# A Hyena convolution as one 512-point transform over even and odd tokens, two channel chunks at once, with token tiles by parity

## Chip, cores and metric

One core of one Trainium2 chip runs the whole program as a single launch. The metric is device time in microseconds (us). The kernel before takes 1788.51 us, the median of 3 runs (1787.72 to 1789.18).

The engines are named as the profile names them: PE (TensorE) multiplies matrices from SBUF into PSUM, DVE (VectorE) and ACT (ScalarE) work element by element, POOL (GpSimd) and SP (SyncE) only issue DMA transfers here; ACT issues some too. Each engine executes its own list of instructions in order and waits at an instruction until what it needs is there.

## The reference

A bidirectional encoder block on 256 tokens of width 2048: one wide projection, a gated linear attention (GLA) branch with 4 heads, a Hyena branch of order 2, their gated sum, an output projection, and a squared-ReLU MLP, all in float32. The change is in the Hyena convolution, and in the order in which tokens lie in the tiles.

```python
def _gla_branch(...):                       # q, k, v, r by heads, decay gates la_f, la_b
    o_f = _gla_one_direction(qh, kh, vh, la_f)
    o_b = flip(_gla_one_direction(flip(qh), flip(kh), flip(vh), flip(la_b)))
    ...
def _short_conv(u, w, b):                   # 3 taps over the tokens, each channel by itself
    ...
def _hyena_branch(u, conv_w, conv_b, ...):
    uc = _short_conv(u, conv_w, conv_b).astype(f32)
    v, x1, x2 = jnp.split(uc, 3, axis=-1)
    h = _hyena_filters(L, ...)              # an MLP over 256 positions, times a decay
    filt = jnp.concatenate([h[:, :, 0], zeros, jnp.flip(h[1:, :, 1], axis=0)], axis=0)
    filt_f = jnp.fft.rfft(filt, axis=0)
    z = v
    for o, gate in enumerate((x1, x2)):
        zf = jnp.fft.rfft(z, n=2 * L, axis=1)
        zc = jnp.fft.irfft(zf * filt_f[None, :, o], n=2 * L, axis=1)[:, :L]
        z = gate * (zc + skip[o] * z)
    return z
```

## The kernel before

**Products.** Every float32 operand is split into a high part (cast on ACT, L90) and a low part (the rest, on DVE, L91), and a product is three matmuls: high x low, high x high, low x high. Weights arrive in blocks of 128x2048 (SP, L104); a block is two halves of 128x1024, each split into `whi` and `wlo`. There are three buffers of each, so ACT and DVE can run three halves ahead of PE. `next_block` takes one block for each step of a product loop.

**Order.** The loop over blocks calls `pump` after every block. `later(d, f)` puts a piece of side work on a list, to be emitted d pumps later; so side work (filters, gates, transforms) is laid between weight blocks. Within that, a scheduler sets the order on each engine at build time; marked pieces get priority or keep their place. An engine's list is then fixed.

**Stages.** In order: opening, q and k; the filter MLP and its spectra, in which the groups r, and the first of v, supply the weight work (about 100 to 265 us); GLA, beside the groups v and g1 (about 265 to 437); Hyena, beside u and go (about 437 to 890); then the gates g2, the outputs, and the MLP from about 1100 us.

**PSUM.** Two pools of four 128x512 banks: `psum_main` holds the two tiles of a token group (`v0_0`, `v0_1` and so on; group and token half), so two groups fit; `psum_side` is for side work.

**Filter stage** (`filt_time`, `filt_freq`; SBUF pool `fp`). There are 16 pairs (c, o): 8 chunks of 256 channels, 2 orders. For each, two matmul groups give `ha` and `hb`, DVE multiplies them by the decay (L433), ACT and DVE split into `hx`, and ACT copies `h0` (L441). `filt_freq` computes the spectra: `X` of even and odd positions as 128x512 products, and a third one, `X0`, from `h0` as 128x256 products (L337, L340, L341 with `eoh`, `eol`). DVE joins them into `T` (L465 to L469), which POOL stores to `Td` in DRAM (L473).

**GLA stage** (pool `gp`, opened when `fp` is closed, and placed in its memory). For each head a group `v` of four blocks; its two PSUM tiles are split at once, with priority, into `yg`, a tile of the base pool. `gla_gates` loads `wr` (ACT's queue, L542), splits it into `ws` (L544, L545) and multiplies `z` (L556); ACT and DVE make the gates.

**Hyena stage** (pool `hp`). For each s of 4 (512 channels) the groups `uv`, `ux1`, `ux2` give v, x1 and x2; `short_conv` multiplies PSUM by the taps (six 512-wide products, L734), adds the bias (L736) and shifts tokens by accumulating DMAs on POOL (L743). Then, for each of the two chunks c of s and each order o: `hy_load` (POOL loads T as `Tl`), `hy_fwd` (transform on PE to `Zp`, ACT copies to `Z`), `hy_mul` (DVE: L785 to L791, then a split), and `hy_inv` (inverse transform to `yp`, gate on DVE, L806, then a split, or the transposes `yT` at the last order).

Of the kernel before, what the change touches and what calls it, by code (L numbers as in the profile page):

```python
# [47 lines left out]
def block_kernel(  # L48
# [301 lines left out]
    def filt_consts():  # L350
        raw = fp.tile([P, 4, P], F32, tag="w4", bufs=2, name="dftraw")
# [22 lines left out]
    def filt_layer(l):  # L374
        def run():
            mw, mc, g = fst["mw"], fst["mc"], fst["g"]
            with tc.high_priority():
# [15 lines left out]
                g2 = fp.tile([P, L], F32, tag="dec", bufs=2, name=f"mlpg{l}")  # L393
# [16 lines left out]
    def filt_time(c, o):  # L410
        def run():
            l1, l2 = fst["l"]
            if o == 0:
                dec = fp.tile([P, NT, CW], F32, tag="dec", bufs=2, name=f"dec{c}")
                nc.scalar.dma_start(dec, decay_in[:, c * CW:(c + 1) * CW].rearrange("(a p) d -> p a d", p=P))
                fst["dec"] = dec
# [6 lines left out]
            nc.scalar.activation(wb, w4[:, 1, :], AF.Copy, scale=sgn_sb[:, 1:2])  # L423
# [13 lines left out]
            hx = fp.tile([P, 2, 2, 2, CW], F32R, tag="hx", bufs=2, name=f"hx{c}{o}")  # L437
            split_hi_lo(hx[:, 0], hx[:, 1], h)
            h0 = fp.tile([P, 2, 2, CW], F32R, tag="h0", bufs=1, name=f"h0_{c}{o}")
            for d in range(2):  # L440
                nc.scalar.copy(h0[d * 64:d * 64 + 64], hx[0:64, :, :, d].bitcast(F32))  # L441
            fst[("h", c, o)] = (hx, h0)
        return run

    def filt_freq(c, o):
        def run():
            hx, h0 = fst.pop(("h", c, o))
            eoh, eol = fst["eo"]
            par_ps = []
            for par in range(2):  # L450
                pt = psum_side(f"X{c}{o}{par}")
                mm3(pt, eoh[:, par], eol[:, par], hx[:, 0, par], hx[:, 1, par], True, True)
                par_ps.append(pt.rearrange("p (a b) -> p a b", a=2))
            xe, xo = par_ps
            t = fp.tile([P, 2, 3, CW], F32, tag="T", bufs=2, name=f"T{c}{o}")
            e, e0 = t[:, 0, 2:0:-1], t[:, 0, 0]
            nc.scalar.copy(e, xe)
# [4 lines left out]
            nc.scalar.copy(e0, p0[:, 0:CW])
            TT = nc.vector.tensor_tensor
            for sg, op in ((1, ALU.subtract), (0, ALU.add)):
                TT(t[:, sg, 2:0:-1], e, xo, op=op)  # L465
            for sg, op in ((1, ALU.subtract), (0, ALU.add)):
                TT(t[:, sg, 0], e0, p0[:, CW:], op=op)
            TT(t[:, :, 2], t[:, :, 2], t[:, :, 0], op=ALU.subtract)
            nc.vector.scalar_tensor_tensor(t[:, :, 1], t[:, :, 1], sgn_sb[:, 0:1], t[:, :, 0],  # L469
                                           op0=ALU.mult, op1=ALU.subtract)  # L470
            td = drp.tile([P, 2, 3, CW], F32, tag=f"T{c}{o}", name=f"Td{c}{o}")
            for ri in range(2):
                nc.gpsimd.dma_start(td.rearrange("(s p) r k c -> r p s (k c)", s=2)[ri],  # L473
                                    t[ri * 64:ri * 64 + 64].rearrange("p s k c -> p s (k c)"))
            T_dram[(c, o)] = td
        return run
# [14 lines left out]
    nc.vector.tensor_tensor(a_sum[:, 0], pa[:, 0], a_low, op=ALU.add)  # L491
# [134 lines left out]
    def gla_scores(h):  # L626
        def run():
# [21 lines left out]
            split_hi_lo(sth, stl, st)  # L649
# [79 lines left out]
    def short_conv(pss, i, tag, name):  # L729
        y = hp.tile([P, NT, 512], F32, tag=tag, bufs=2 if tag == "x2" else 1, name=name)  # L730
# [28 lines left out]
    def hy_load(c, o):
        def run():  # L760
            t = hp.tile([P, 2, 3, CW], F32, tag="Tl", name=f"Tl{c}{o}")
            nc.gpsimd.dma_start(t, T_dram[(c, o)])
            cst[("T", c, o)] = t
        return run

    def hy_fwd(c, o):
        def run():
            t = cst.pop(("T", c, o))
            zh, zl = cst.pop(("z", c, o))
            z = hp.tile([P, 3, 2, CW], F32, tag="Z", name=f"Z{c}{o}")  # L770
            for ri in range(2):
                pz = psum_side(f"Zp{c}{o}{ri}")
                mm3(pz.rearrange("p (a b) -> p a b", a=2), dfth[:, ri], dftl[:, ri], zh, zl, True, True, hold=True)
                nc.scalar.copy(z[:, 2:0:-1, ri, :], pz.rearrange("p (a b) -> p a b", a=2))
            cst[("Z", c, o)] = (t, z)
        return run

    def hy_mul(c, o):
        def run():
            t, z = cst.pop(("Z", c, o))  # L780
            a = hp.tile([P, 3, 2, CW], F32, tag="pa", name=f"pa{c}{o}")
            b = hp.tile([P, 3, 2, CW], F32, tag="pb", name=f"pb{c}{o}")
            TT = nc.vector.tensor_tensor
            full = [P, 3, 2, CW]
            TT(z[:, 0], z[:, 1], z[:, 2], op=ALU.add)  # L785
            TT(a, z, t[:, 0, :, None, :].broadcast_to(full), op=ALU.mult)
            TT(b, z[:, :, ::-1, :], t[:, 1, :, None, :].broadcast_to(full), op=ALU.mult)
            TT(a[:, :, 0], a[:, :, 0], b[:, :, 0], op=ALU.subtract)
            TT(a[:, :, 1], a[:, :, 1], b[:, :, 1], op=ALU.add)
            y = a[:, 1:3]  # L790
            TT(y, y, a[:, 0:1].broadcast_to([P, 2, 2, CW]), op=ALU.add)  # L791
            yh = hp.tile([P, 2, 2, CW], F32R, tag="pb", name=f"Yh{c}{o}")
            yl = hp.tile([P, 2, 2, CW], F32R, tag="Yl", name=f"Yl{c}{o}")
            split_hi_lo(yh, yl, y)
            cst[("Y", c, o)] = (yh, yl)
        return run

    def hy_inv(c, o):
        def run():
            yh, yl = cst.pop(("Y", c, o))  # L800
            py = psum_side(f"yp{c}{o}")
            py3 = py.rearrange("p (a b) -> p a b", a=2)
            mm3(py3, dfth[:, 2], dftl[:, 2], yh[:, :, 0], yl[:, :, 0], True, False)
            mm3(py3, dfth[:, 3], dftl[:, 3], yh[:, :, 1], yl[:, :, 1], False, True)
            zf = hp.tile([P, NT, CW], F32, tag="zf", name=f"zf{c}{o}")
            nc.vector.tensor_tensor(zf, py3, gate_part(("x1", "x2")[o], c), op=ALU.mult)  # L806
            if o == 0:
                z = tuple(hp.tile([P, NT, CW], F32R, tag=t, name=f"{t}{c}") for t in ("zh", "zl"))
                split_hi_lo(z[0], z[1], zf)
                cst[("z", c, 1)] = z  # L810
            else:
                pt = psum_side(f"yT{c}")
                for cc in range(2):
# [821 lines left out]
```

## Time and profile before

| what | us |
|---|---|
| median of the runs | 1788.51 |
| span of the profiled execution | 1785.8 |
| PE busy | 1778.0 |
| DVE busy | 1482.7 |
| ACT busy | 1052.2 |
| POOL busy | 180.0 |

The median lies 2.7 us above the span; the difference is what lies around the profiled program. A row of the groups reads: line, engine, operation, output and inputs by name (partitions by elements, type), count, then the busy time, the mean time of one in ns, and the idle time of the engine just before it with what ended it. A row of the timeline begins with start and duration in us; `x2` joins two instructions, and an idle time stands in brackets. A row of the windows gives the stretch, its length, the busy time of PE, weight loads, DVE, ACT and POOL with the instructions in brackets, PE's granted clock, the share of DMA time and GB/s. Busy times of neighbouring instructions overlap on PE and DVE, so the pace, from start to start, is shorter than the duration.

### The profile page before, as it was taken

Reading aid. Unit: us, or ns where it says so; the run is one execution under the profiler, and the core shown is the slowest. Engines: PE = TensorE matmul, PEld = TensorE weight load, DVE = VectorE, ACT = ScalarE, POOL = GpSimd, SP = SyncE. Lnnn points to the kernel's source line nnn. Section 1 sums busy time; section 2 is a strip of 40 time slices with the busy share of each in tenths; the row PEclk is TensorE's granted clock in tenths of the full one; section 3 lists DMA queues with packets and bytes.
Section 4 is the critical chain, followed back from the end, with each engine's and each line's share of the span. In section 5 each row is a group of like instructions: output and inputs, shape, how many; then the busy total and the mean of one; then the engine's idle time right before and its main releaser. Section 6 shows DMA issues by size and latency. Waiting matters only on the chain.

```text
span 1785.8 us, 23513 instructions
## 1 busy us (share of the span) xinstructions
PE 1778.0 (100%) x8739; PEld 1500.6 (84%) x8739; DVE 1482.7 (83%) x1919; ACT 1052.2 (59%) x1418; POOL 180.0 (10%) x234
## 2 busy tenths in 40 slices
PE   9999999999999999999999999999999999999998
PEld 7888888888888888888888889888888888888887
DVE  6789886885679998898755558889999999999998
ACT  6578767875344444444544445676666666666663
POOL 1011110000011201011000000011111111111110
PEclk9999999999999999999999999999999999999999
DMA  8668776445797979798555664687888787888864
GB/s 325 236 241 292 262 233 202 148 165 206 230 288 254 290 232 292 262 289 253 215 184 186 245 263 163 224 247 242 276 248 252 246 264 241 278 240 249 262 217 167
DMA packets 81586, 428.95 MB, mean 240 GB/s; under 512 B 10072, under 2 KB 12648, under 8 KB 40768
## 3 DMA queue, kind: packets, MB, share of 16 engines
q1 hardware_dynamic: 47664, 336.35, 50.5%
q0 software_dynamic: 26608, 71.18, 19.6%
q10 hardware_dynamic: 7200, 19.93, 3.1%
q8 instruction: 68, 1.11, 0.3%
q14 instruction: 46, 0.38, 0.1%
HBM read 383.96 MB, written 16.25 MB: 224 GB/s over the span
## 4 chain that ended last, share of the span: by engine, by line
PE 96%; DVE 3%; DMA 0%; issue 0%; ACT 0%; SPq 0%; DVEq 0%
PE f L151 12%; PE f L155 6%; PE w L1266 5%; PE w L1265 5%; PE w L1264 5%; PE g L202 3%; PE g L201 3%; PE g L203 3%; PE ux L203 3%; PE ux L202 3%; PE ux L201 3%; PE r L201 2%; PE r L203 2%; PE r L202 2%; PE k L151 2%; PE v L202 2%
## 5 line engine op out<-in xcount | busy, mean ns | idle before, releaser
L90 ACT CAST whi<-raw 128x1024 fp32r<-128x1024 f32 x360 | 379.1, 1054 | 382.6 <-PE ux L203 89.3
L91 DVE TENSOR_TENSOR wlo<-raw,whi 128x1024 fp32r<-128x1024 f32 x360 | 438.0, 1220 | 186.5 <-ACT whi L90 183.4
L151 PE MATMUL f<-hT,whi 128*128 128x512 f32 x984 | 243.9, 391 | 0.0
L151 PEld LDWEIGHTS f<-hT,whi 128*128 128x128 f32 x984 | 180.8, 188 | 35.0
L1122 DVE TENSOR_TENSOR wlo<-fraw,whi 128x1024 fp32r<-128x1024 f32 x112 | 136.7, 1221 | 14.3 <-ACT whi L1125 11.0
L155 PEld LDWEIGHTS f<-hT,wlo 128*128 128x128 f32 x984 | 126.2, 191 | 4.8
L155 PE MATMUL f<-hT,wlo 128*128 128x256 f32 x984 | 127.7, 283 | 0.0
L1125 ACT CAST whi<-ring 128x1024 fp32r<-128x1024 f32 x56 | 59.1, 1055 | 113.1 <-DVE ring L1122 113.1
L1185 POOL DMA_DIRECT2D ring<-wblk x56 | 48.6, 868 | 722.6 <-DVE ring L1122 722.6
L1125 ACT CAST whi<-fraw 128x1024 fp32r<-128x1024 f32 x112 | 117.7, 1051 | 0.0
L1125 ACT CAST b_h<-ring 128x1024 fp32r<-128x1024 f32 x112 | 87.9, 834 | 24.0 <-PE w L1266 21.9
L202 PE MATMUL g<-wlo,xT 128*128 128x512 f32 x256 | 100.1, 391 | 0.0
L203 PE MATMUL ux<-whi,xT 128*128 128x512 f32 x256 | 99.9, 390 | 0.0
L203 PE MATMUL g<-whi,xT 128*128 128x512 f32 x256 | 99.9, 390 | 0.0
L202 PE MATMUL ux<-wlo,xT 128*128 128x512 f32 x256 | 99.6, 389 | 0.0
L201 PE MATMUL g<-whi,xT 128*128 128x512 f32 x256 | 93.8, 392 | 0.0
L201 PE MATMUL ux<-whi,xT 128*128 128x512 f32 x256 | 89.7, 389 | 0.0
L1122 DVE TENSOR_TENSOR ring<-ring 128x512 f32<-128x512 f32 x112 | 77.0, 687 | 1.9
L1122 DVE TENSOR_TENSOR b_l<-ring,b_h 128x1024 fp32r<-128x1024 f32 x56 | 68.3, 1219 | 9.1 <-ACT b_h L1125 9.0
L1122 DVE TENSOR_TENSOR wlo<-ring,whi 128x1024 fp32r<-128x1024 f32 x56 | 68.6, 1224 | 2.6 <-ACT whi L1125 0.6
L1122 DVE TENSOR_TENSOR fa<-ring,fa 128x1024 fp32r<-128x1024 f32 x56 | 68.2, 1217 | 0.0
L1186 POOL DMA_DIRECT2D ring<-ring x56 | 67.6, 1207 | 0.0
(515 smaller groups left out, 4299.5 us busy)
## 6 DMA issues: line engine op xcount, KB each, us to landing
raw<-wblk SPq DMA_DIRECT2D x188, 1024.0 KB, 5.3
fraw<-wblk SPq DMA_DIRECT2D x56, 1024.0 KB, 4.8
ring<-wblk SPq DMA_DIRECT2D x56, 1024.0 KB, 6.7
ring<-wblk POOLq DMA_DIRECT2D x56, 256.0 KB, 4.4
ring<-ring POOLq DMA_DIRECT2D x56, 256.0 KB, 5.0
Td<-T POOLq DMA_DIRECT2D x32, 384.0 KB, 5.4
conv_sb<-conv_rows SPq DMA_DIRECT2D x12, 1024.0 KB, 11.5
Tl<-Td POOLq DMA_DIRECT2D x16, 768.0 KB, 9.2
```

Of the source, the lines that this page charges most:

```text
L90: return (nc.scalar.copy(hi, src), nc.vector.tensor_tensor(lo, src, hi.bitcast(F32), op=ALU.subtract))
L91: nc.vector.tensor_tensor(lo, src, hi.bitcast(F32), op=ALU.subtract))
L151: MM(ps[:, :, ts], hi[:, js], act[:, kt, :, ts], start=(kt == 0 and opens), stop=(kt == KT - 1))
L155: MM(ps[:, 0, ts], lo[:, js], act[:, kt, 0, ts], start=False, stop=False)
L201: order(MM(pss[tb], sh, wh, start=(kt == ends[0]), stop=False))
L202: order(MM(pss[tb], sh, wl, start=False, stop=False))
L203: order(MM(pss[tb], sl, wh, start=False, stop=(kt == ends[1])))
L1122: return pin(nc.vector.tensor_tensor(dst, a, b, op=op))
L1125: return pin(nc.scalar.copy(hi, src))
L1264: pin(MM(ps, sh, wh, start=(p == begin), stop=False))
L1265: MM(ps, sh, wl, start=False, stop=False)
L1266: pin(MM(ps, sl, wh, start=False, stop=(p == end - 1)))
```

## The change

The 512-point transform of a sequence of 256 tokens is now taken as one transform over even tokens and one over odd tokens (`Ze`, `Zo`), whose sum and difference are the two halves of the spectrum. The filter's spectrum is built from taps modulo 4: four products of 128x256 for each pair, in place of two of 128x512 and two of 128x256 (each of three matmuls). One T holds each spectrum for both halves of the frequencies, for two chunks, as one tile of 1 MB, so 8 loads of 1 MB take the place of 16 of 768 KB. The Hyena steps work on 512 channels at once: each is called 8 times, for (s, o), and was called 16 times, for (c, o).

For this, the token tiles lie by parity: tile 0 holds even tokens, tile 1 odd ones, from the input on. GLA needs tokens in order, so the sums of q, k and a are written in order by a stride, and each head's v takes a new way: ACT copies PSUM to `vm`, POOL's queue moves it by four transfers to `vr` in order, and the split into `yg` follows two pumps later. The scores are turned to parity order in their split. x2 and the decay have one buffer where there were two; the filter's multiplication by the decay is one product of 1024; the products with T are 2048 wide.

```diff
@@ filt_time
-            h = fp.tile([P, 2, 2, CW], F32, tag="h", bufs=1, name=f"h{c}{o}")
-            for par, pp in ((0, pa), (1, pb)):
-                nc.vector.tensor_tensor(
-                    h[:, par], pp.rearrange("p (a b) -> p a b", a=2),
-                    dec[:, par, None, :].broadcast_to([P, 2, CW]), op=ALU.mult,
-                )
...
+            nc.scalar.copy(h[top, 1:4:2], pa[top])
+            nc.scalar.copy(h[end, 1:4:2], pa[end, ::-1])
+            for r, src in ((0, top), (2, end)):
+                for d, dst in enumerate((top, end)):
+                    nc.scalar.copy(h[dst, r], pb[src, d])
+            nc.vector.tensor_tensor(h, h, dec, op=ALU.mult)
...
@@ filt_freq
+            near, far = (psum_side(f"X{c}{o}{i}").rearrange("p (a c) -> p a c", a=2) for i in range(2))
+            for ps, r0 in ((near, 0), (far, 2)):
+                for i in range(2):
+                    mm3(ps[:, i], eoh[:, r0 + i], eol[:, r0 + i], hx[:, 0, r0 + i], hx[:, 1, r0 + i], True, True)
+            f = fp.tile([P, 2, CW], F32, tag="F", name=f"F{c}{o}")
+            nc.scalar.copy(f, near)
+            TT = nc.vector.tensor_tensor
+            u = fp.tile([P, 4, CW], F32, tag="U", name=f"U{c}{o}")
+            TT(u[:, 0:4:2], f, far, op=ALU.add)
+            TT(u[:, 1], f[:, 0], far[:, 0], op=ALU.subtract)
+            TT(u[top, 3], f[end, 1], far[end, 1], op=ALU.subtract)
+            TT(u[end, 3], far[top, 1], f[top, 1], op=ALU.subtract)
+            t = fp.tile([P, 2, 2, CW], F32, tag="T", bufs=2, name=f"T{c}{o}")
+            TT(t[:, :, 0], u[:, 0:2], u[:, 2:4], op=ALU.add)
+            TT(t[:, :, 1], u[:, 0:2], u[:, 2:4], op=ALU.subtract)
...
@@ the heads' v
+        mixed = gp.tile([P, NT, 512], F32, tag="vm", name=f"vm{h}")
         with tc.high_priority():
             for tb in range(NT):
-                split_hi_lo(vh[:, tb], vl[:, tb], pss[tb])
-        v_sb[h] = (vh, vl)
+                nc.scalar.copy(mixed[:, tb], pss[tb])
+        rows = gp.tile([P, NT, 512], F32, tag="vr", name=f"vr{h}")
+        for b in range(NT):
+            for tb in range(NT):
+                nc.gpsimd.dma_start(rows[tb:P:2, b], mixed[b * 64:(b + 1) * 64, tb])
+
+        def split(h=h, vh=vh, vl=vl, rows=rows):
+            split_hi_lo(vh, vl, rows)
+            v_sb[h] = (vh, vl)
+        later(2, split)
@@ short_conv
-        y = hp.tile([P, NT, 512], F32, tag=tag, bufs=2 if tag == "x2" else 1, name=name)
+        y = hp.tile([P, NT, 512], F32, tag=tag, name=name)
...
-            (y[1:P], past[0:P - 1]),
-            (y[0:1, 1], past[P - 1:P, 0]),
-            (y[0:P - 1], ahead[1:P]),
-            (y[P - 1:P, 0], ahead[0:1, 1]),
+            (y[:, 1], past[:, 0]),
+            (y[1:P, 0], past[0:P - 1, 1]),
+            (y[:, 0], ahead[:, 1]),
+            (y[0:P - 1, 1], ahead[1:P, 0]),
...
@@ hy_fwd, hy_mul, hy_join, hy_split, hy_inv
+            for ri in range(2):
+                even, odd = psum_side(f"Ze{s}{o}{ri}"), psum_side(f"Zo{s}{o}{ri}")
+                for ps, i in ((even, 0), (odd, 1)):
+                    mm3(ps, dfth[:, 2 * i + ri], dftl[:, 2 * i + ri], zh[:, i], zl[:, i], True, True, hold=True)
+                e = b[:, ri, 0:512]
+                nc.scalar.copy(e, even)
+                for k, op in enumerate((ALU.add, ALU.subtract)):
+                    nc.vector.tensor_tensor(x[:, ri, :, k], halves_of(e), halves_of(odd), op=op)
...
+            for dst, src, ri in ((a, x, 0), (b, x[:, ::-1], 1)):
+                nc.vector.tensor_tensor(dst, src, t[:, ri:ri + 1].broadcast_to([P, 2, 1024]), op=ALU.mult)
...
+            TT(a[:, 0], a[:, 0], b[:, 0], op=ALU.subtract)
+            TT(a[:, 1], a[:, 1], b[:, 1], op=ALU.add)
+            y = a.rearrange("p r (h k c) -> p (r h) k c", h=2, k=2)
+            w = hp.tile([P, 2, 4, CW], F32, tag="X", name=f"W{s}{o}")
+            for i, op in enumerate((ALU.add, ALU.subtract)):
+                TT(w[:, i], y[:, :, 0], y[:, :, 1], op=op)
...
@@ the Hyena loop
-                steps = [(2 * s + j % 2, j // 2, 4 * j) for j in range(4)]
-                for c, o, d in steps:
-                    later(7 + d, hy_load(c, o))
-                    later(9 + d, hy_fwd(c, o))
-                for c, o, d in steps:
-                    later(13 + d, hy_inv(c, o))
-                for c, o, d in steps:
-                    later(9 + d, hy_mul(c, o))
+                for o in range(2):
+                    for d, step in ((5, hy_load), (8, hy_fwd), (9, hy_mul), (10, hy_join), (12, hy_split), (14, hy_inv)):
+                        later(d + 8 * o, step(s, o))
```

Three places show how the lists of the engines move.

PE where the filter stage ends. Before, the last spectrum's products (`X710`, `X711`, their third part `X071`) stand inside block 37, in the second group of v:

```order
L201 MATMUL v1_1_2678<-whi37_1_2582,xT_82 128x512
L337 MATMUL X710_2155<-hx71_2071,eoh_351 128x512
L340 MATMUL X710_2155<-hx71_2071,eoh_351 128x512
L341 MATMUL X710_2155<-hx71_2071,eol_352 128x512
L337 MATMUL X711_2159<-hx71_2071,eoh_351 128x512
...
L203 MATMUL v1_1_2678<-whi37_1_2582,xT_82 128x512
L337 MATMUL X071_2165<-h0_71_2074,eoh_351 128x256
L340 MATMUL X071_2165<-h0_71_2074,eoh_351 128x256
...
L201 MATMUL v1_0_2677<-whi37_1_2582,xT_82 128x512
```

After, the spectrum of that pair stands behind the whole second group of v, directly ahead of the third group, `v2`:

```order
L208 MATMUL v1_1_2706<-whi40_1_2747,xT_82 128x512
L209 MATMUL v1_1_2706<-wlo40_1_2748,xT_82 128x512
L210 MATMUL v1_1_2706<-whi40_1_2747,xT_82 128x512
L344 MATMUL X710_2180<-hx71_2099,eoh_351 128x256
L347 MATMUL X710_2180<-hx71_2099,eoh_351 128x256
L348 MATMUL X710_2180<-hx71_2099,eol_352 128x256
...
L344 MATMUL X711_2181<-hx71_2099,eoh_351 128x256
...
L348 MATMUL X711_2181<-hx71_2099,eol_352 128x256
L208 MATMUL v2_0_3001<-whi41_0_2872,xT_82 128x512
```

The last spectrum moved down by about three and a half weight blocks, from inside group v1 to its end.

ACT at the same place. Before, the casts that free the PSUM tiles of v0 (`yg` from `v0_0` and `v0_1`) stand ahead of the copies of the last T; the casts for v1 come after the scan and gate loads (`scan_sb`, `wr`) and several halves of weights:

```order
L90 CAST yg_2406<-v0_0_2413 128x512
L90 CAST yg_2406<-v0_1_2414 128x512
L90 CAST whi38_0_2612<-raw38_2610 128x1024
L90 CAST whi38_1_2616<-raw38_2610 128x1024
L457 COPY T71_2163<-X710_2155 128x2x256
L462 COPY T71_2163<-X071_2165 128x256
...
L531 DMA scan_sb_2409<-scan_in 128x260
L542 DMA wr0_2449<-wa2 128x512
...
L544 CAST ws0_2451<-wr0_2449 128x512
...
L90 CAST yg_2406<-v1_0_2677 128x512
L90 CAST yg_2406<-v1_1_2678 128x512
```

After, the spectrum's copy `F71` is followed by the copies of group v0 out of PSUM, then the scan and gate loads, then the copies of group v1:

```order
L90 CAST whi42_0_2961<-raw42_2959 128x1024
L462 COPY F71_2194<-X710_2180 128x512
L695 COPY vm0_2697<-v0_0_2437 128x512
L695 COPY vm0_2697<-v0_1_2438 128x512
L533 DMA scan_sb_2433<-scan_in 128x260
L544 DMA wr0_2473<-wa2 128x512
L546 CAST ws0_2475<-wr0_2473 128x512
L544 DMA wr1_2775<-wa2 128x512
L695 COPY vm1_2993<-v1_0_2705 128x512
L695 COPY vm1_2993<-v1_1_2706 128x512
L90 CAST yg_2430<-vr0_2700 128x1024
L90 CAST whi42_1_2965<-raw42_2959 128x1024
```

The rows that free the PSUM tiles of v0 moved from before the last spectrum to behind it, and the gate loads and the next half of weights behind them.

DVE in the Hyena stage, between two halves of weights (`wlo`). Before, around the second chunk's products of order 1 (`pa11`, `pb11`) and the convolution of x2:

```order
L786 TENSOR_TENSOR pa11_5324<-Z11_5297,Tl11_5212 128x1536
L787 TENSOR_TENSOR pb11_5325<-Z11_5297,Tl11_5212 128x1536
L91 TENSOR_TENSOR wlo91_1_5270<-raw91_5263,whi91_1_5269 128x1024
L788 TENSOR_TENSOR pa11_5324<-pa11_5324,pb11_5325 128x3x256
L789 TENSOR_TENSOR pa11_5324<-pa11_5324,pb11_5325 128x3x256
L91 TENSOR_TENSOR wlo92_0_5339<-raw92_5336,whi92_0_5338 128x1024
L791 TENSOR_TENSOR pa11_5324<-pa11_5324 128x1024
L91 TENSOR_TENSOR wlo92_1_5343<-raw92_5336,whi92_1_5342 128x1024
...
L734 TENSOR_TENSOR cx21_5447<-ux21_0_5261,conv_sb_4257 128x512
L734 TENSOR_TENSOR shift_4258<-ux21_0_5261,conv_sb_4257 128x512 x2
...
L91 TENSOR_TENSOR wlo94_0_5416<-raw94_5413,whi94_0_5415 128x1024
...
L736 TENSOR_TENSOR cx21_5447<-cx21_5447,conv_sb_4257 128x1024
```

After, around the products of (1, 0) and the convolution of x2:

```order
L91 TENSOR_TENSOR wlo94_0_5439<-raw94_5436,whi94_0_5438 128x1024
L790 TENSOR_TENSOR X10_5470<-pb10_5471,Zo100_5473 128x2x256 x2
...
L801 TENSOR_TENSOR pa10_5544<-X10_5470,Tl10_5338 128x2048
L801 TENSOR_TENSOR pb10_5471<-X10_5470,Tl10_5338 128x2048
L91 TENSOR_TENSOR wlo94_1_5443<-raw94_5436,whi94_1_5442 128x1024
L746 TENSOR_TENSOR cx21_5496<-ux21_0_5302,conv_sb_4305 128x512
...
L746 TENSOR_TENSOR shift_4306<-ux21_0_5302,conv_sb_4305 128x512
...
L91 TENSOR_TENSOR wlo95_0_5513<-raw95_5510,whi95_0_5512 128x1024
L809 TENSOR_TENSOR pa10_5544<-pa10_5544,pb10_5471 128x1024
L810 TENSOR_TENSOR pa10_5544<-pa10_5544,pb10_5471 128x1024
L748 TENSOR_TENSOR cx21_5496<-cx21_5496,conv_sb_4305 128x1024
L91 TENSOR_TENSOR wlo95_1_5517<-raw95_5510,whi95_1_5516 128x1024
```

The products are 2048 wide instead of 1536 and stand with four adds ahead of them; between `wlo94_0` and `wlo95_1` stand the adds, the products, the six products of the convolution, two joins and the bias add.

More of the change, by code (lines that the diff above doesn't have):

```diff
@@ L446, in run @@
         def run():
-            hx, h0 = fst.pop(("h", c, o))
+            hx = fst.pop(("h", c, o))
             eoh, eol = fst["eo"]
[L449 to L455, printed above, removed]
@@ L466, in run @@
[L466 to L471, printed above, removed]
+            top, end = slice(0, 64), slice(64, P)
+            near, far = (psum_side(f"X{c}{o}{i}").rearrange("p (a c) -> p a c", a=2) for i in range(2))
@@ L752, in run, with halves_of @@
-            for i in range(2):
-                cst[("z", 2 * s + i, 0)] = tuple(t[:, :, i * CW:(i + 1) * CW] for t in z)
-        return run
-    def gate_part(n, c):
-        return cst[(n, c // 2)][:, :, c % 2 * CW:(c % 2 + 1) * CW]
-    def hy_load(c, o):
+            t = hp.tile([P, 2, 1024], F32, tag="Tl", name=f"Tl{s}{o}")
+            nc.gpsimd.dma_start(t, T_dram[(s, o)].rearrange("p r h s c -> p r (h s c)"))
+            cst[("T", s, o)] = t
+        return run
+    def halves_of(ap):
+        return ap.rearrange("p (h c) -> p h c", h=2)
@@ new lines, in hy_fwd, with run @@
+    def hy_fwd(s, o):
+        def run():
+            zh, zl = cst.pop(("z", s, o))
+            x = hp.tile([P, 2, 2, 2, CW], F32, tag="X", name=f"X{s}{o}")
+            b = hp.tile([P, 2, 1024], F32, tag="pb", name=f"pb{s}{o}")
+            for ri in range(2):
[6 more added lines that the diff above has]
+                    nc.vector.tensor_tensor(x[:, ri, :, k], halves_of(e), halves_of(odd), op=op)
+            cst[("X", s, o)] = (x, b)
+        return run
@@ new lines, in hy_split, with run, hy_inv @@
+    def hy_split(s, o):
+        def run():
+            w = cst.pop(("W", s, o)).rearrange("p i (r h) c -> p (i r) (h c)", r=2)
+            yh, yl = (hp.tile([P, 4, 512], F32R, tag=t, name=f"{n}{s}{o}") for t, n in (("pb", "Yh"), ("pa", "Yl")))
+            split_hi_lo(yh, yl, w)
+            cst[("Y", s, o)] = (yh, yl)
+        return run
+    def hy_inv(s, o):
+        def run():
+            yh, yl = cst.pop(("Y", s, o))
+            g = cst.pop((("x1", "x2")[o], s))
+            for i in range(2):
+                py = psum_side(f"yp{s}{o}{i}")
+                for ri in range(2):
+                    k = 2 * i + ri
+                    mm3(py, dfth[:, 4 + k], dftl[:, 4 + k], yh[:, k], yl[:, k], ri == 0, ri == 1)
+                nc.vector.tensor_tensor(g[:, i], py, g[:, i], op=ALU.mult)
+            if o == 0:
+                split_input(s, 1, g)
+            else:
+                for i in range(2):
+                    later(1 + 2 * i, hy_turn(2 * s + i, g[:, :, i * CW:(i + 1) * CW]))
+        return run
@@ L760, in run, with hy_turn @@
+    def hy_turn(c, zf):
         def run():
[L761 to L813, printed above, removed]
-                    for tb in range(NT):
-                        nc.tensor.transpose(pt[:, cc * L + tb * P:cc * L + (tb + 1) * P], zf[:, tb, cc * P:(cc + 1) * P], ident)
-                pt = pt.rearrange("p (a b) -> p a b", a=2)
-                if c >= NCH - 2:
-                    split_hi_lo(yhT[:, 2 * c:2 * c + 2, 0], yhT[:, 2 * c:2 * c + 2, 1], pt)
-                    return
-                yo = base.tile([P, 2, L], F32, tag="sum", name=f"yo{c}")
-                nc.scalar.copy(yo, pt)
-                def keep():
-                    yd = drp.tile([P, 2, L], F32, tag=f"yd{c}", name=f"yd{c}")
-                    nc.gpsimd.dma_start(yd, yo)
-                    yh_dram[c] = yd
-                later(1, keep)
@@ new lines, in run @@
+            pt = psum_side(f"yT{c}")
+            for cc in range(2):
+                for tb in range(NT):
+                    nc.tensor.transpose(pt[:, cc * L + tb * P:cc * L + (tb + 1) * P], zf[:, tb, cc * P:(cc + 1) * P], ident)
+            pt = pt.rearrange("p (a b) -> p a b", a=2)
+            if c >= NCH - 2:
+                split_hi_lo(yhT[:, 2 * c:2 * c + 2, 0], yhT[:, 2 * c:2 * c + 2, 1], pt)
+                return
+            yo = base.tile([P, 2, L], F32, tag="sum", name=f"yo{c}")
@@ L828, in hy_inv, with keep @@
+            nc.scalar.copy(yo, pt)
+            def keep():
+                yd = drp.tile([P, 2, L], F32, tag=f"yd{c}", name=f"yd{c}")
+                nc.gpsimd.dma_start(yd, yo)
+                yh_dram[c] = yd
+            later(1, keep)
         return run
@@ L1603, in _layout @@
     emb = np.zeros((P, L), f)
-    by_parity = np.concatenate([np.arange(0, L, 2), np.arange(1, L, 2)])
-    emb[:33] = emb[64:97] = e.T[:, by_parity]
+    emb[:33] = emb[64:97] = e.T[:, times]
     dl = np.abs(np.linspace(math.log(1e-2) / 1.5, math.log(1e-2) / 0.3, D, dtype=f))
-    decay = np.exp(-t * dl[None, :]).astype(f)[by_parity]
+    decay = np.exp(-t * dl[None, :]).astype(f)
+    decay = np.stack([decay[abs(np.concatenate(rows[r]))] for r in range(4)], axis=1)
     up = np.triu(np.ones((64, 64), np.int32))
```

125 lines of the change are left out of this document (70 added, 55 removed).

## The prediction

> **What bounds the kernel now.** I read the page's first and fourth parts, then the view of waits for TensorE, then the table of windows by stage.
>
> ```profile
> span 1785.8 us, 23513 instructions
> PE 1778.0 (100%) x8739; PEld 1500.6 (84%) x8739; DVE 1482.7 (83%) x1919; ACT 1052.2 (59%) x1418; POOL 180.0 (10%) x234
> PE 96%; DVE 3%; DMA 0%; issue 0%; ACT 0%; SPq 0%; DVEq 0%
> ...
> PE warm L272 <- DVE ones_sb L334: 1.5, 1, 1.5
> PE open L296 <- ACT whi-1_2_133 L308: 0.9, 1, 0.9
> ...
> 437.00:880.00 443.00, 443.00 (x1967) 366.72 (x1966) 374.91 (x374) 201.41 (x220) 54.74 (x74) 1.00 0.83 263
> 265.00:437.00 172.00, 172.00 (x851) 143.26 (x850) 124.94 (x241) 125.92 (x258) 1.77 (x3) 1.00 0.51 179
> 100.00:265.00 165.00, 165.00 (x771) 137.09 (x770) 147.33 (x200) 121.72 (x155) 18.03 (x30) 1.00 0.77 262
> ```
>
> TensorE (PE) is busy for the whole span and the chain runs through it for 96%. The two waits listed are all that it has, 2.4 us in the opening. In the filter stage (100 to 265 us), the GLA stage (265 to 437) and the Hyena stage (437 to 880; these three hold the change) it is busy in every microsecond at a granted clock of 1.00. So the time is TensorE's work, and the rule for the sum is simple: a matmul removed is worth its pace; anything removed from DVE, ACT or the DMA queues is worth nothing; and anything that makes TensorE wait costs all of that wait. DVE at 374.91 of 443 us is 85% of the Hyena stage, so bursts matter there, not averages. The profiled span is 1785.8 us and the median of the runs 1788.5, so 2.7 us lie around the span; the sum is made on the span and these are added.
>
> **TensorE's own work.** The paces come from the chain, where rows stand start to start, and the counts from the groups by form.
>
> ```profile
> 63.31 1.91 PE k L155 x16
> 65.22 3.65 PE k L151 x16
> ...
> L337 PE MATMUL X<-hx,eoh 128*128 128x512 f32 x32 | 12.7, 397 | 0.0
> L337 PE MATMUL X<-h,eoh 128*128 128x256 f32 x32 | 9.0, 280 | 0.0
> ```
>
> Sixteen 256-column matmuls take 1.91 us (0.1195 each), sixteen of 512 take 3.65 (0.228; 0.2265 between undisturbed starts). The spectrum of a filter pair was 6 matmuls of each size (three lines, 32 of each in all); it becomes 12 of 256. That is 6 x 16 x (0.2265 - 0.1195) = **10.3 us less**. Everything else on TensorE keeps its columns: the transform was two 512-wide products over two chunks and is now two over even and odd tokens at twice the width half as often. 1785.8 - 10.3 = 1775.5 is the floor.
>
> **Filter stage, DVE.**
>
> ```profile
> L465 DVE TENSOR_TENSOR T<-T,X 128x512 f32<-128x512 f32 x32 | 21.8, 681 | 1.7 <-ACT T L457 1.4
> L91 DVE TENSOR_TENSOR hx<-h,hx 128x1024 fp32r<-128x1024 f32 x16 | 19.5, 1219 | 0.5 <-ACT hx L90 0.5
> L467 DVE TENSOR_TENSOR T<-T,X 128x256 f32<-128x256 f32 x32 | 13.3, 415 | 4.7 <-ACT T L462 4.4
> L469 DVE SCALAR_TENSOR_TENSOR T<-T,sgn_sb 128x512 f32<-128x512 f32 x16 | 11.9, 745 | 0.0
> L468 DVE TENSOR_TENSOR T<-T 128x512 f32<-128x512 f32 x16 | 11.0, 687 | 0.2
> ```
>
> By those sizes a pair loses two 512 products (1.36) for one of 1024 (1.22), and 2 x 0.681 + 2 x 0.415 + 0.687 + 0.745 = 3.62 becomes three of 512 and three of 256 elements, 3.29. DVE gets 0.5 us a pair lighter while TensorE gets 0.64 lighter: its load stays near 147.33 of 165 us, and I expect no wait from it. ACT's small copies replace two 1.05 us casts; its cover is 121.72 of 165. Cost taken: 0.
>
> **The joint between filter and GLA stage.** Here the change's new copy is decisive. The value tiles were split straight from PSUM into a base tile; now they are first copied into vm, a tile of the GLA pool, which takes memory of the filter pool. That copy must wait until the last spectrum T has been stored by DMA. Before, only an unimportant DVE instruction waited for this:
>
> ```profile
> 265.51 0.74 DVE L469 SCALAR_TENSOR_TENSOR T<-T,sgn_sb 128x512 f32<-128x512 f32 x1
> ...
> 266.55 1.20 POOL L473 DMA_DIRECT2D Td<-T  x2 [12.67 <-DVE T L469]
> ...
> 272.24 0.17 DVE L534 TENSOR_SCALAR nba_sb<-ba_sb 128x16 f32<-128x16 f32 x1 [2.22 <-DMA Td<-T]
> ...
> 272.66 0.46 ACTq L542 DMA_DIRECT2D wr<-wa  x1
> ...
> 277.92 0.62 ACT L544 CAST ws<-wr 128x512 fp32r<-128x512 f32 x1 [3.66 <-DMA wr<-wa]
> ...
> DMA to landing us min/median/max: 3.6/5.4/8.7
> ```
>
> From the end of T (266.25) to the first instruction that the landing lets through (272.24) are 6.0 us, 0.3 of them to the issue; the last row, of the Td stores, gives 3.6 to 8.7 for the landing. In the new order the copies of v0 out of PSUM stand on ACT behind F71 and that wait; TensorE's next tile v2_0 needs v0's PSUM buffer (four buffers: v0, v1). The last spectrum's matmuls stand directly ahead of v2_0, after all of v1: there is nothing left to run under the wait.
>
> With t = 0 at the start of X710: twelve matmuls, TensorE free at 1.43. F71 is copied by 1.8; DVE does wlo42_0 until 2.5, then U71 (0.6 + 3 x 0.335) until 4.1 and T71 (2 x 0.6) until 5.3. (0.6 and 0.335 are 681 and 415 ns less the 80 ns by which neighbours overlap.) The landing comes 5.9 later, at 11.2, the copy (580 ns for 512 elements, as L457 takes below) ends at 11.8, and v2_0 starts at 11.9.
>
> ```profile
> L457 ACT COPY T<-X 128x512 f32<-128x512 f32 x16 | 9.3, 580 | 6.0 <-DMA Td<-T 5.2 <-PE X L341 0.7
> ```
>
> **Wait: 11.9 - 1.43, about 10.4 us**; bounds 9.0 to 14.1 by landings of 3.6 and 8.7 against the 5.0 of this one (its second store was issued at 267.15). What is late next stands behind the same copies on ACT: scan, wr0, ws0, wr1, vm1, yg, whi42_1. wr0 is issued at 12.7 and lands 5.2 later (272.66 to 277.92), ws0 is ready at 19.3, and z00, which TensorE reaches after 26 products at 17.8, waits 1.6. vm1, yg and whi42_1 follow until 22.5, wlo42_1 until 24.0 against 22.35 wanted: 1.7. ws1 waits for wr1, so wlo43_0 comes at 28.1 against 26.7: 1.4. These **follow-ups are 4.7 us**, bounds 0 (a fast landing of wr0 and ACT catching up) to 6.
>
> The clock: in the tail of this run, where TensorE's last matmul ends at about 1780.5, the records show the clock falling.
>
> ```profile
> 1782.00:1786.00 4.00, 0.00 (x0) 0.00 (x0) 0.00 (x0) 0.00 (x0) 0.00 (x0) 0.67 0.42 130
> ```
>
> A mean of 0.67, if it fell to one half, means a fall near 1783.3, some 3 us into idleness (an estimate from this row). So the 10.4 us wait should end at a lower clock. I add nothing for it: v2_0 and its neighbours run slower, but they only run up to z00, which has 1.6 us to wait anyway. The Trainium skill ("TensorE: Matmul & The Clock Gate", in "Part 1: The HAM clock gate", "What's actually happening") puts the fall at an idle window of about 3.4 us and the return to full rate after about 3.4 us of busy time; by it the first 3.4 us at half rate would cost an estimated 1.7 us, hence at most 0.1 us more than that wait hides.
>
> The sixteen vr copies go through POOL's queue at about 0.6 us each; 1.77 of 172 us of POOL and half of the DMA time are used in the GLA stage, and their split comes two weight blocks (10.9 us) later, against 2.4 us of issues and 5.4 of landing. Cost taken: 0, bound 2.
>
> **Hyena stage.** DVE must deliver a half weight block (wlo) every 2.72 us (12 x 0.2265), and TensorE has three halves in buffers. What decides is how much other work stands between two deliveries. Rows of the stage before:
>
> ```profile
> 540.83 1.75 DVE L786 TENSOR_TENSOR pa<-Z,Tl 128x1536 f32<-128x1536 f32 x1
> 542.49 1.75 DVE L787 TENSOR_TENSOR pb<-Z,Tl 128x1536 f32<-128x1536 f32 x1
> 544.16 0.68 DVE L91 TENSOR_TENSOR zl<-zf,zh 128x512 fp32r<-128x512 f32 x1
> 544.76 1.22 DVE L91 TENSOR_TENSOR wlo<-raw,whi 128x1024 fp32r<-128x1024 f32 x1
> 545.90 0.95 DVE L788 TENSOR_TENSOR pa<-pa,pb 128x768 f32<-128x768 f32 x1
> ...
> 549.91 1.22 DVE L91 TENSOR_TENSOR wlo<-raw,whi 128x1024 fp32r<-128x1024 f32 x1
> ...
> 552.57 0.39 PE L202 MATMUL uv<-wlo,xT 128*128 128x512 f32 x1
> ```
>
> Paces are 1.66 (1536), 1.14 (1024) and 0.60 (512). The half that ends at 551.13 is first used at 552.57: 1.44 us to spare, near the least of the stage, after a burst of 512 + 512 + 2 x 1536 + 512. The change has less DVE work in sum (13312 elements of transform work for each s instead of 15360) but twice as much at a time: four adds, two products of 2048, four joins of 1024. A 2048-wide product appears in no row; between 1.66 (1536) and 2.27 (two of 1024) I take 2.20, on the line through 1024 and 1536.
>
> For s = 1, 2, 3 with o = 0 the order puts adds and products, then six convolution products, then two joins and the bias add between neighbouring halves. t = 0 at the first Ze product: TensorE needs 2.72 for Ze and Zo, 5.43 for block 93, 0.44 for the transposes yT1, 5.44 for block 94, and wants wlo95_0 at 14.26. DVE: wlo94_0 until 2.45, adds (4 x 0.6) 4.85, products (4.4) 9.25, wlo94_1 10.4, convolution (6 x 0.6) 14.0, wlo95_0 15.1, with the semaphore 15.3: **1.0 late**. Joins and bias (3 x 1.14) and wlo95_1 until 19.8 against 18.0: **1.8 late**. With 0.3 for rounding at the two hand-overs, 3.1 us three times, 9.3. At (0,0) and at o = 1 of s = 0, 1, 2 the same sum with convolution, adds and products gives a half at about 15.2 against 14.3, 0.85 us four times, 3.4. At (3,1) no convolution stands near: 0. **Hyena sum 12.7 us**; with products at 1.66 each burst is 1.1 lighter (6.0 left at the three places, none at the four), with 2.27 about 1 us more in all.
>
> **Sum.** 1785.8 - 10.3 + 10.4 + 4.7 + 12.7 = 1803.3 us of span, plus 2.7: **1806 us**. Its own bounds: low terms 9.0 + 0 + 6.0 give 1793.2, high ones 14.1 + 6 + 2 + 13.7 give 1814.0.
>
> **Rivals.**
> 1. *The bursts are covered.* The three buffered halves swallow them: DVE runs ahead further than my sum lets it. For it: 1.44 us to spare is the worst row shown of before; against it: before's largest excess of DVE over TensorE across three halves is 3.5 us by my paces, the new one 8.9, and the buffers give about 5.9. Time 1806 - 12.7 = 1793.
> 2. *Not slower: the joint does not hold TensorE.* One mechanism: if the last Td store lands before v0's copy is due, ACT frees the PSUM buffer at once and the queue behind it is on time. Price 10.4 + 4.7, time 1791, within 0.2%. It decides if the landing comes within about 1.4 us of X711, that is before DVE could even have finished T71 at 5.3; the row of 3.6 us at best speaks against it.
> 3. *Only the removed matmuls count.* Rivals 1 and 2 together: 1778. TensorE's order and the idle shares of DVE (15%) and ACT (over 40%) speak for it, the two walks against it.
> 4. *More waits than I see*: the filter's pairs are stretched over four more weight blocks with one buffer for decay and h, so an ACT or DVE wait could reach TensorE in the filter stage too, or the clock stays low through the three follow-ups: 10 us more, 1816 and above.
>
> **How the numbers follow.** Forecast 0.60, of which all is slower; rival 1 0.12 (0.05 of it inside the band, the rest slower), rival 2 0.09 (0.07 inside), rival 3 0.11 (faster), rival 4 0.08. A difference of 0.2% is about what a measurement of this kernel can tell from none, so the band is 1784.9 to 1792.1. Faster 0.11, same 0.12, slower 0.77. The range leaves out rival 3 and the far part of rival 4: 1788 to 1817.
>
> **What would show it.** Right: the view of waits lists TensorE on v2_0 waiting for ACT's vm copy, once, about 10 us, the clock below 1.00 behind it; small waits on z00, whi42_1 and wlo43_0; and in 437 to 890 us some ten waits of 0.5 to 2 us for wlo. X groups show 192 matmuls of 256 columns. Wrong: TensorE still at 100% busy in the Hyena windows (rival 1), no wait at v2_0 (rival 2), or waits in 100 to 265 us (rival 4).

## The result, and the profile after

The changed kernel takes 1802.06 us, the median of 4 runs (1801.57 to 1802.23), against 1788.12 us for the kernel before on the same chip. The ratio is 1.0076, with a 95% interval of 1.0062 to 1.0091: **slower by 13.9 us**. The forecast was 1806 us, within 1788 to 1817.

The page of the changed kernel:

```profile
span 1800.2 us, 23526 instructions
PE 1774.5 (99%) x8739; PEld 1495.6 (83%) x8739; DVE 1460.3 (81%) x1871; ACT 1051.7 (58%) x1442; POOL 185.2 (10%) x242
```

The view of waits of its TensorE (PE); the columns are engine and line, what it waited for, us in total, times, the longest:

```profile
PE v L208 <- ACT vm L695: 9.6, 1, 9.6
PE go L209 <- DVE wlo L91: 7.0, 7, 1.5
PE ux L209 <- DVE wlo L91: 1.7, 3, 0.6
...
PE g L209 <- DVE wlo L91: 0.4, 1, 0.4
...
PE v L209 <- DVE wlo L91: 0.4, 1, 0.4
```

PE is no longer busy throughout. DVE's busy time fell from 1482.7 to 1460.3 us, which bought nothing. PE's own went from 1778.0 to 1774.5 only, although the spectra became 11 us cheaper. The windows show where PE idles, and a part of why its busy time fell so little:

```profile
264.00:270.00 6.00, 5.74 (x32) 4.80 (x30) 3.02 (x4) 2.65 (x3) 0.00 (x0) 1.00 0.73 217
...
272.00:274.00 2.00, 0.00 (x0) 0.00 (x0) 1.76 (x4) 0.00 (x0) 0.00 (x0) 0.96 0.10 41
274.00:276.00 2.00, 0.00 (x0) 0.00 (x0) 0.00 (x0) 0.00 (x0) 1.20 (x2) 0.50 0.41 88
...
280.00:282.00 2.00, 2.00 (x6) 1.55 (x5) 0.00 (x0) 0.02 (x1) 1.61 (x4) 0.50 0.96 287
282.00:284.00 2.00, 2.00 (x6) 1.58 (x5) 0.68 (x1) 0.60 (x1) 0.00 (x0) 0.50 0.44 154
284.00:286.00 2.00, 2.00 (x10) 1.59 (x10) 0.00 (x0) 1.71 (x3) 0.00 (x0) 0.98 0.42 131
```

PE idles from 269.75 to 279.31. The granted clock is at 0.50 from just before 274, and still for 4.8 us after PE has resumed: from 280 to 284 PE counts as fully busy but the row counts 6 matmuls in each 2 us, and 10 in the 2 us behind them. A busy share doesn't show such a loss; the clock beside it does. PE's timeline over the same stretch:

```profile
279.31 0.79 PE L208 MATMUL v<-whi,xT 128*128 128x512 f32 x1 [9.56 <-ACT vm L695]
...
280.32 0.63 PE L210 MATMUL v<-whi,xT 128*128 128x512 f32 x1
280.75 0.63 PE L208 MATMUL v<-whi,xT 128*128 128x512 f32 x1
...
284.14 0.39 PE L210 MATMUL v<-whi,xT 128*128 128x512 f32 x1
284.37 0.39 PE L208 MATMUL v<-whi,xT 128*128 128x512 f32 x1
```

Eleven matmuls start in the 4.83 us up to 284.14, 0.43 apart, then 0.23 apart; at full pace they take 2.49, so 2.3 us are lost. (By the means of 0.96 and 0.98 the clock fell 4.1 us into the idle time and rose 4.8 us after its end, estimates from these rows. The Trainium skill, in "TensorE: Matmul & The Clock Gate", "What's actually happening", asks for at least one idle window of about 3.4 us before the fall and at least one busy window of that length before the rise, and says that the windows run freely; 4.1 and 4.8 us agree with that.)

The timeline of the joint, a start and a duration first in each row, an idle time in brackets:

```profile
273.12 0.68 DVE L471 TENSOR_TENSOR T<-U 128x512 f32<-128x512 f32 x1
274.10 1.20 POOL L477 DMA_DIRECT2D Td<-T  x2 [12.02 <-DVE T L471]
278.53 0.17 DVE L536 TENSOR_SCALAR nba_sb<-ba_sb 128x16 f32<-128x16 f32 x1 [4.72 <-DMA Td<-T]
278.67 0.59 ACT L695 COPY vm<-v 128x512 f32<-128x512 f32 x1 [8.63 <-issue]
...
279.07 0.46 ACTq L544 DMA_DIRECT2D wr<-wa  x1
...
281.98 0.62 ACT L546 CAST ws<-wr 128x512 fp32r<-128x512 f32 x1 [2.24 <-DMA wr<-wa]
```

This is the forecast chain: T ends at 273.80, its store lands at 278.53, the copy of v0 starts at 278.67, and v2_0 at 279.31. In this timeline ACT's wait is marked "issue"; DVE's nba_sb, let through at the same moment, names the landing, and so does the view of the tile Td, where the copy stands among those that waited for the store:

```profile
  ACT vm L695: 8.6, 1
```

That the copy waits because vm lies in memory of the closed filter pool is read from the code: vm and T have nothing else to do with each other. No run put vm elsewhere. wr0 then came in 2.9 us, where it had taken 5.2 before.

DVE in one of the three bursts of the Hyena stage (s = 1, o = 0), and the two late halves behind it (a late half is a half weight block whose wlo is not ready when PE wants it):

```profile
615.04 2.29 DVE L801 TENSOR_TENSOR pa<-X,Tl 128x2048 f32<-128x2048 f32 x1
617.25 2.28 DVE L801 TENSOR_TENSOR pb<-X,Tl 128x2048 f32<-128x2048 f32 x1
619.45 1.22 DVE L91 TENSOR_TENSOR wlo<-raw,whi 128x1024 fp32r<-128x1024 f32 x1
620.58 1.28 DVE L746 TENSOR_TENSOR cx<-ux,conv_sb 128x512 f32<-128x512 f32 x2
621.78 2.47 DVE L746 TENSOR_TENSOR shift<-ux,conv_sb 128x512 f32<-128x512 f32 x4
624.17 1.22 DVE L91 TENSOR_TENSOR wlo<-raw,whi 128x1024 fp32r<-128x1024 f32 x1
...
625.44 0.50 PE L209 MATMUL go<-wlo,yg 128*128 128x512 f32 x1 [0.64 <-DVE wlo L91]
...
629.99 0.50 PE L209 MATMUL go<-wlo,yg 128*128 128x512 f32 x1 [1.51 <-DVE wlo L91]
```

DVE works without a gap through all its rows here and delivers the half at 625.39; PE takes it at 625.44, after 0.64 us of idle time, and the next half after 1.51.

Each wait costs PE more than its idle time, since the start before it and the one behind it are stretched too. So the balance is made from start to start: the time from each matmul's start to the next one's, added up over the 8739 matmuls of both traces by the name of the output. The groups that differ by more than 0.4 us:

```
                     before    after   difference (us)
X                     33.66    32.19      -1.47   (of the after, 9.72 is the wait behind the last X)
v                     87.43    90.52      +3.08
g1, g2               175.67   176.79      +1.11
go                    87.12    96.59      +9.47
ux                   174.51   177.19      +2.68
s (128x64)             6.93     7.45      +0.53
w                    304.71   305.33      +0.62
r                     87.97    87.55      -0.41
```

So X itself saves 33.66 - 22.47 = 11.2 us; the wait at v2_0 costs 9.7, what follows it 3.1 (v) + 0.5 (s, the scores) and about 1 in g1, and the Hyena stage 12.15 (go and ux).

### The profile page after: what moved, and what is told of

Its sections match the earlier page's. It is cut to its first block, busy times and chain, and to the rows that moved or that the text cites. A ratio compares the mean times of both kernels' runs of the same rounds, so it can differ in the third digit from the quotient of the medians.

```text
span 1800.2 us, 23526 instructions
## 1 busy us (share of the span) xinstructions
PE 1774.5 (99%) x8739; PEld 1495.6 (83%) x8739; DVE 1460.3 (81%) x1871; ACT 1051.7 (58%) x1442; POOL 185.2 (10%) x242
## 4 chain that ended last, share of the span: by engine, by line
PE 88%; DVE 9%; issue 2%; ACT 1%; DMA 0%; DVEq 0%; ACTq 0%
PE f L151 12%; PE f L155 6%; PE w L1295 5%; PE w L1294 5%; PE w L1293 5%; PE g L209 3%; PE g L210 3%; PE g L208 3%; PE ux L209 3%; PE ux L210 3%; PE ux L208 2%; DVE wlo L91 2%; PE k L151 2%; PE r L210 2%; PE r L209 2%
```

## The experiments

The kernel before took 1788.12 us beside the changed kernel, 1788.30 beside the runs with 20/15, 19/15, a product left out and the finer steps, and 1788.67 beside the others. So a difference to the changed kernel's 1802.06 us holds to about half a microsecond.

**The joint: the filter pairs laid closer.** Two kernels, with

```diff
-        n = 4 + (i * 21) // 15
+        n = 4 + (i * 20) // 15
```

and with 19 in place of 20. The last spectrum then stands 34 and 46 matmuls (7.7 and 10.4 us) ahead of v2_0; 46 are a little less than two weight blocks of 24, not more as expected.

> The 16 filter pairs are laid at steps of 20/15 weight blocks instead of 21/15, so the last spectrum stands about one block (some 34 matmuls, 7.7 us of TensorE work) ahead of v2_0; nothing else changes. Theory (the joint wait is the chain last spectrum -> T -> store -> landing -> vm copy, a fixed length of about 10 to 11 us): the wait at v2_0 shrinks from 9.6 us to 2 to 3.5 us, the granted clock stays at 1.00 since the idle time is then shorter than the 4 us after which it fell, and the time falls by 8 to 10 us to about 1793. Rival (the copies wait for something tied to the GLA stage, such as the vr transfers or the pool's opening, not for the last spectrum): the wait stays near 9.6 us and the time within 2 us of 1802.

> Like the run with 20/15, but with steps of 19/15 blocks, the last spectrum more than two blocks ahead of v2_0. Theory: no wait at v2_0, the clock at 1.00 throughout, no follow-ups over 1 us: 12 us less, about 1790. Rival: the closer filter pairs fill DVE and ACT in the filter stage, and waits of TensorE for wlo or whi appear there (before 265 us) that give back more than 3 us: 1793 or more.

With 20/15: 1788.85 us, a ratio of 1.0005 (0.9995 to 1.0014) to the kernel before. With 19/15: 1791.54 us, 1.0017 (1.0008 to 1.0026). PE's wait at the joint and the releasing rows, first with 20/15, then with 19/15:

```profile
265.38 1.20 POOL L477 DMA_DIRECT2D Td<-T  x2 [11.21 <-DVE T L471]
...
269.87 0.59 ACT L695 COPY vm<-v 128x512 f32<-128x512 f32 x1 [2.30 <-DMA Td<-T]
...
270.51 0.50 PE L208 MATMUL v<-whi,xT 128*128 128x512 f32 x1 [1.31 <-ACT vm L695]
```

```profile
263.47 1.20 POOL L477 DMA_DIRECT2D Td<-T  x2 [12.04 <-DVE T L471]
264.33 19.66 SPq L104 DMA_DIRECT2D raw<-wblk  x4
...
271.62 0.59 ACT L695 COPY vm<-v 128x512 f32<-128x512 f32 x1 [3.24 <-DMA Td<-T]
...
272.26 0.50 PE L208 MATMUL v<-whi,xT 128*128 128x512 f32 x1 [2.25 <-ACT vm L695]
```

The theory holds with 20/15: the wait follows the last spectrum, from 9.6 to 1.3 us, and the clock stays at 1.00. The fall of 13.2 us was more than the 8 to 10 expected, since the slow stretch and the late halves behind the joint went too (v is 1.4 us cheaper even with the new wait counted in it, g 1.1, s 0.6). The expectation for 19/15 was wrong in the wait and its rival was wrong in the place: it still waits 2.3 us at v2_0, and nowhere in the filter stage. Here the store, issued at 263.47, let the copy go at 271.62, 8.15 us later against 4.5 with 20/15. The weight load on SP's queue went out at 264.33, right behind it; with 20/15 none was issued for 3.5 us after the store. That the two shared the transfer engines is likely, and was not tried by itself. The second halves of all 160 stores of a T in the ten traces speak for it: of 31 that had a weight load issued at most 0.5 us behind them, the landing took 5.7 to 8.7 us from the issue, 7.0 in the median; of 81 that had none for 2.5 us, 3.6 to 7.2, 5.0 in the median. Of the 2.7 us between the two runs, this longer wait is 1.0; of the rest the profiles show 0.5 in the opening, which the edit doesn't touch.

**The clock: matmuls put into the wait.**

```diff
+            if (c, o) == (NCH - 1, 1):
+                idle = psum_side("idle")
+                for _ in range(40):
+                    tc.keep_in_program_order(MM(idle, xT[:, 0, 0, 0:P], xT[:, 0], start=True, stop=True))
             f = fp.tile([P, 2, CW], F32, tag="F", name=f"F{c}{o}")
```

> The changed kernel with 40 matmuls of 128x512 that nobody reads put between the last spectrum and v2_0 (9.1 us at full pace), in the time in which TensorE waits; the scheduler moves whi42_1 ahead of the vm1 copies. It does extra work and takes away the idle time, not the wait. Theory (the wait costs its length and, beside it, some 2 us because eleven matmuls behind it run at half the pace): the granted clock stays at 1.00, v2_0 starts at the same 279 us, the 26 matmuls from v2_0 to z00 take 5.9 us where they took 8.3, and the time falls by 1 to 2.5 us to about 1800. Rival (the slow stretch only fills a wait that comes anyway, for ws0 or whi42_1): a wait of 1.5 to 2.5 us appears at z00 or behind it, and the time stays within 0.7 us of 1802.

1798.16 us, 3.9 below the changed kernel (1 to 2.5 were expected), with the 40 matmuls as extra work; the ratio to before is 1.0057 (1.0043 to 1.0070). PE's timeline:

```profile
269.30 9.25 PE L464 MATMUL idle<-xT 128*128 128x512 f32 x40
279.02 0.50 PE L208 MATMUL v<-whi,xT 128*128 128x512 f32 x1 [0.46 <-ACT vm L699]
```

and the window that holds the joint:

```profile
262.00:290.00 28.00, 27.54 (x129) 22.73 (x128) 12.76 (x16) 11.17 (x17) 3.94 (x8) 1.00 0.58 172
```

v2_0 starts when it did, the clock stays at 1.00, and v as a group is 2.0 us cheaper. So the slow stretch was a cost of its own and filled no other wait. g and s got cheaper by 1.8 us as well; the order behind the joint differs here (whi42_1 ahead of the vm1 copies), so that part can't be put down to the clock.

**The Hyena stage: one product left out.** The second product with T is not computed, and the joins read the spectrum itself:

```diff
-            for dst, src, ri in ((a, x, 0), (b, x[:, ::-1], 1)):
+            for dst, src, ri in ((a, x, 0),):
...
-            cst[("ab", s, o)] = (a, b)
+            cst[("ab", s, o)] = (a, x)
```

> The second 2048-wide product of the Hyena transform (spectrum with the other half of T) is left out, and the joins take the unmultiplied spectrum in its place: 8 products of 2.28 us less on DVE, 17.6 us of pace. Theory (only halves that come late cost): at the four places (0,0) and o = 1 of s = 0, 1, 2 the delay of 0.8 us is gone, since 2.2 us are taken out of the burst; at the three places o = 0 of s = 1, 2, 3 the joins move up into the gap, ahead of the convolution, so the two waits there stay, 2.5 to 3.3 us a place. Time 3 to 4 us below 1802. Rival (DVE's throughput over the stage is what counts): about 10 us or more below, with all the waits gone.

1798.23 us, 3.8 below the changed kernel. DVE's busy time over the whole span is 1443.3 us, where it was 1460.3, and PE's waits from 440 to 890 us are

```profile
PE go L209 <- DVE wlo L91: 6.6, 6, 1.5
```

The group ux waits no more (it had 1.7 us in 3 waits), of go's seven waits the six at o = 0 of s = 1, 2, 3 remain; from start to start the two groups are 3.3 us cheaper. Taking 17 us of work from DVE bought 3.8 us, as expected: only what stands in front of a late half counts.

**The Hyena stage: the same work laid finer.** The two parts of the transform as two steps a block apart, each followed by its products of 1024, and the later steps one block on:

```diff
-                    for d, step in ((5, hy_load), (8, hy_fwd), (9, hy_mul), (10, hy_join), (12, hy_split), (14, hy_inv)):
+                    for d, step in ((5, hy_load), (8, lambda s, o: hy_fwd(s, o, 0)), (9, lambda s, o: hy_mul(s, o, 0)), (9, lambda s, o: hy_fwd(s, o, 1)), (10, lambda s, o: hy_mul(s, o, 1)), (11, hy_join), (13, hy_split), (15, hy_inv)):
```

> The same DVE work in the Hyena stage, laid out finer: the forward transform of real and imaginary part as two steps one block apart, each followed at once by its two products of 1024 (four of 1024 for two of 2048), joins, split and inverse a block later. DVE work rises by about 0.07 us for each product cut. Theory (waits come from what stands between two wlo halves): the waits in 440 to 900 us fall from 11.9 us to 5 to 7.5 us, the time to 1795 to 1798. Rival (they come from the amount of DVE work, or from the convolution being held by the transposes of the chunk before through the single x2 buffer): waits unchanged, time 1801 to 1804.

1793.49 us, a ratio of 1.0032 (1.0019 to 1.0045) to before, and 8.6 us below the changed kernel; better than expected. DVE's products take 38.9 us where they took 36.6, and its busy time over the whole span is 1460.4 us against 1460.3: no less work, but fewer waits. What the view of waits still lists there:

```profile
PE uv L208 <- ACT whi L90: 1.4, 2, 0.7
PE g L208 <- ACT whi L90: 0.7, 1, 0.7
```

Now it is ACT's half that comes late, once for each of s = 1, 2, 3: the first cast of a block, right behind the burst. From start to start each of these costs 1.0 us; a wlo for go that comes 0.15 us late behind each, too little for that view, costs another 0.4. go is 4.7 us and ux 3.1 us cheaper from start to start, uv 0.3 dearer: 12.15 us of loss became 4.7. The run changes two things at once, the smaller pieces and the later steps, and doesn't tell which of them took the waits away.

**Both remedies, and a control.** The spread steps with filter pairs at 18/15 and at 17/15; and the kernel before with 18/15.

> Both remedies: the Hyena steps spread as in the run before, and the filter pairs at steps of 18/15 blocks, which puts the last spectrum 58 matmuls (13.1 us) ahead of v2_0. With steps of 19/15 the chain from the end of the last spectrum to v2_0 took 12.8 us (8.4 of it the landing), with 20/15 9.2 us. Theory: no wait or under 1 us at v2_0, the clock at 1.00; of the change there remain the 11 us saved on the spectra and some 4 to 5 us of waits in the Hyena stage: 1793.5 less 12 to 14, 1779 to 1782, faster than the kernel before. Rival (the closer pairs now make TensorE wait in the filter stage): 1784 or more.

> As the run with 18/15, with steps of 17/15 blocks, the last spectrum some 85 matmuls ahead of v2_0: surely no wait there even for the longest landing seen. Theory: same time as with 18/15 within 1 us, unless the filter stage itself runs short: DVE then has about 0.96 of TensorE's time there, and waits for wlo before 265 us would show as 1 to 5 us more.

> The kernel before, unchanged but for filter pairs at steps of 18/15 instead of 21/15. Its TensorE never waited at the joint, so there is nothing to gain: within 1 us of 1788.3. Rival (closer pairs help by themselves, whatever the change did): 2 us or more faster.

With 18/15: 1781.18 us, a ratio of 0.9964 (0.9951 to 0.9976) to before, **faster than both kernels** and within what was expected. No wait at v2_0; the copies are let through at 265.29, while PE still works on v1. With 17/15: 1786.1 us, a ratio of 0.9989 (0.9979 to 0.9998), 4.9 us more. Its waits for wlo up to 262 us, of which the run with 18/15 has none:

```profile
PE r L209 <- DVE wlo L91: 2.1, 1, 2.1
PE v L209 <- DVE wlo L91: 0.7, 1, 0.7
```

A third one, of 1.0 us, follows in v at 285.9. With 18/15 the wait at v2_0 was gone already, so the still closer pairs save nothing and cost these waits; the step was expected to be level, unless DVE ran short, and it did. The kernel before with 18/15 takes 1789.3 us, 1.0003 (0.9994 to 1.0012): the spacing by itself is worth nothing, it only takes back what the change lost.

## Why the prediction was right, and where not

The sign, the size and the places held; of the sum each term:

- **Spectra: 10.3 forecast, 11.2 measured.** The count was right, the pace a little low: X runs at its own paces. Six of 512 take 260.52 to 261.92 in the trace of before, 0.233 each, and not 0.2265; twelve of 256 after the change take 0.117 each.

```profile
260.52 0.24 PE X L337
...
261.92 0.23 PE v L202
```

- **The wait at v2_0: 10.4 forecast, 9.6 measured**, by the very chain that was written down. T took 4.05 us from TensorE's end instead of 3.9, the landing 4.7 instead of 5.9.
- **Follow-ups: 4.7 forecast at three named places; about the same sum by another way.** This is the step that failed. z00 did not wait at all, because wr0 landed in 2.9 us and not in 5.2, so the argument that the slow clock would only fill z00's wait, and so cost nothing, fell with it: the eleven slow matmuls cost 2.3 us in full. whi42_1 was not late either: its cast, at 287.31, even waited 1.00 us for PE to give its buffer back. That the slow stretch gave ACT this time is likely and not tried. wlo43_0 waited 0.4 us (0.64 from start to start) and not 1.4. What was not forecast at all is a late half in g1, 0.4 us, and 0.5 us in the scores. That the sum of the follow-ups agrees with the forecast is luck. I had taken one landing as a fixed price; it is the least certain number of such a chain.
- **Hyena: 12.7 forecast, 12.15 measured.** At the three places 0.8 + 0.1 and 1.67 + 0.1 us beyond the pace, 2.7 with small change (3.1 forecast); at the four others 0.83 (0.85 forecast). The price of the 2048-wide product, which no row of before showed, was 2.28 us with a pace of 2.21 (615.04 to 617.25), where 2.20 was taken. At (3,1) nothing waited, as said, and ten waits of 0.6 to 1.5 us in the stage are the "some ten" of the forecast. The 13312 and 15360 elements of transform work are those of each (s, o), not of each s as the prediction has it; the sum doesn't use them.

Rivals 1 and 2 fell with the waits at their places. Rival 4 was right only in that the clock mattered. Added up, the terms gave 17.5 us; PE's last matmul ended 15.1 us later than before (1780.47 and 1795.55), and the span grew by 14.4.

## What to carry to other kernels

Where one engine is busy throughout, count its work, and then look only for places where another engine or a landing can come late: less work elsewhere is worth nothing, and the same work in larger pieces can cost. A tile that moves into a pool opened late can have to wait for transfers of the pool whose memory it takes, as vm did for the last store; if the copy into that tile is what frees a PSUM buffer, the matrix engine waits for the transfer too. Before giving up a change that loses to such a wait, move the work that starts the chain: here a number in a spacing rule and a finer split turned 14 us lost into 7.5 us won.

## What the runs showed of the hardware

The same store of one T took 4.5 us to let its reader go in one run and 8.15 in another, with the difference of where a weight load was issued beside it.

The clock, once down, stayed at half for 4.8 us of full work, so an idle time of 9.6 us cost 11.9. These times are not fixed: the runs with one product left out and with the finer steps have the same wait, of 9.5 and 9.6 us, and by the means of their windows (0.69 in 274 to 276 us and 0.86 in 272 to 274 on the way down, 0.76 in 284 to 286 and 0.58 in 282 to 284 on the way up) the clock fell 5.1 and 3.9 us into it and rose 5.8 and 4.6 us after its end, estimates like those above. From fall to rise it was about 10.2 us in all three. Idle times of 1.3 and 2.3 us at the same place left it at 1.00.
